# The gating unit's first mixes one product later, and another order of the output's block products, in a conditioned MLA and spatial gating layer

## The chip, the cores and the metric

The kernel runs on one core of one Trainium2 chip. What is measured is device time in microseconds (us) for one launch. Each profile is one execution on that chip. Its engines are called here by the names that the profile uses: PE is TensorE's matmuls, PEld its weight loads, DVE is VectorE, ACT is ScalarE, POOL is GpSimd, SP is SyncE, which issues most of the transfers. Times within the profile count from the first instruction.

## The reference

One layer of a decoder trunk for 512 tokens of width 2048, in float32:

```python
h = rmsnorm(x, attn_norm_g) * (1 + scale) + shift          # scale, shift, gate = silu(c) @ w_ada + b_ada
proj = h @ w_in                                            # 2048 x 13632, cut into
q_lat, kv_lat, k_rope, z_mla, u, v, z_sgu, g_mla, g_sgu    # 768, 512, 64 and six times 2048 columns
y_mla = attention(q_lat, kv_lat, k_rope) * silu(z_mla)     # 16 heads, causal, rotary
mixed = einsum('gts,bnsgd->bntgd', tril(w_spatial), rmsnorm(v) in chunks of 128 tokens) + b_spatial
y_sgu = u * mixed * silu(z_sgu)                            # 16 groups of 128 channels
merged = sigmoid(g_mla) * y_mla + sigmoid(g_sgu) * y_sgu
out = rmsnorm(x + gate * (merged @ w_out), final_norm_g)
```

Two places matter for this change: `mixed`, one 128 x 128 product for each group and chunk, and the last product, `merged @ w_out`, 512 x 2048 by 2048 x 2048, with the residual sum and the final norm behind it.

## The kernel before, in words

Every float32 product is made of three matmuls. Each operand is split into a high part (a copy that is rounded to the matmul's type, a cast on ScalarE) and a low part (the difference, on VectorE); high by high, high by low and low by high are summed in a bank of PSUM (`mm3`, lines 184 to 187). So every tile of weights is loaded, cast and subtracted before its matmuls, and the program writes out by hand in which order each engine does that.

**Four stages** follow each other: the first columns of the projection and the conditioning; the columns of v; the gates (266 block products); attention head by head; and the output product.

**Seven products in place of eight.** The v columns, the gates and half of the output's columns are computed with a scheme of seven block products over a cut into two by two blocks. The products are numbered 1 to 7. Products 1, 2, 3 and 4 are accumulated in one set of banks, in the order 1, 2, 3, 4, and copied out between (what is in the banks after each is needed); 6 and 7 in another; 5 in its own. Some weight operands are sums of blocks. Where a sum is not made on VectorE, a transfer makes it: it loads a block and adds it to what lies in the buffer. Such accumulating transfers are issued by POOL, plain loads by SP.

**The gates' stage.** A loop runs over 266 slots, one block product in each. Before it, a planner puts every other step into a slot and a phase (`on`, `place`, lines 817 to 840): a list of FIRST, EVAC, GATE, SPLIT and BACK steps is issued ahead of the slot's matmuls, MISC and LOAD behind them. Steps with a free choice are given a cost in us, and `place` takes the next slot whose sum on VectorE stays under a limit. The split of a slot's weights is issued two slots ahead. The gating unit's mix of two groups is a chain over several slots (lines 1078 to 1095): the spatial weights, their bias and the columns of v are loaded at `s_ - 3`; POOL zeroes the upper triangle at `s_ - 1` (`sgu_weights`, line 1057); ScalarE scales v by its norm (`sgu_scale`, line 1062), which needs `rv`, made in slot 4; PE makes the four products (`sgu_mix`, line 1067, in phase MISC); VectorE takes them from PSUM and adds the bias (`sgu_out`, line 1073). The first pair of groups planned is 14 and 15 (`p` = 7), at slots 1 to 12. Its neighbours in the queues: the accumulation for product 4 of the first pair of gates is issued by POOL in slot 3, phase LOAD, and is used in slot 9; small steps for the rotary angles (`rope_make`) are placed from slot 4 on; the conditioning's dot products (`gate_dot`) from two slots behind the pair's end; and so on through the stage.

**The output's stage.** Columns 1024 to 2047 are made first, plainly, in 16 granules of weights. Columns 0 to 1023 are made with products 1 to 7, four granules of weights for each product. `Stream` (from line 57) holds the list of all granules in the order of use. At each `get` it issues the low part of the next granule, the cast of the one after that, and then as many transfers, in the order of the list, as there are free buffers; it stops at the first that has none, or whose `after` granule has not been split. A granule's buffer is free when its low part has been issued. The buffers for plain loads are three, a fourth (`k0`, `k1`) from step 16 to step 24, and another (`ys2`) from step 27. A granule of product 3 is one load and one accumulation onto the same buffer (`both`). A granule of product 6, 2 or 4 has no buffer of that kind: product 6 uses a chain tile `ch0` to `ch3`, and a granule of 2 or 4 is that chain tile after one more accumulation (`chain_add`). All those accumulations are issued on POOL when the stream comes to them.

The steps 16 to 39 of the loop (from line 1980) are the 24 block products, each with 12 matmuls (`out_block`, line 1876; PE's lines there are called L1883). Copies of banks and the epilogue's steps hang on step numbers (`at_out`). Three of them: `hold` copies product 6's banks at step 23, the sum of 1 and 2 at step 31 (`y12`) and the sum of 1, 2 and 3 at step 35 (`y123`), each on ScalarE, line 1891; the next product on these banks has to wait until they are read. Product 5's first two granules are loaded early into other tiles and split at steps 26 and 27; its last two come through the stream. Product 5 is made last, for two rows of 128 tokens, the second cut into halves, in banks 2, 3 and 6 (`last_product`), while VectorE, ScalarE and POOL finish the other two rows.

## Time and profile before

| | |
|---|---|
| median of 3 runs | 1535.6 us (1534.37 to 1535.95) |
| the profiled execution, its own time | 1538.92 us |
| its span, from the first to the last instruction | 1537.2 us |
| mean granted PE clock | 0.997 of full speed |
| PE busy | 1517.3 us, 99% |
| PEld busy | 1412.9 us, 92% |
| VectorE busy | 1244.6 us, 81% |
| ScalarE busy | 808.6 us, 53% |
| POOL busy | 135.4 us, 9% |
| transfers | 346.48 MB, mean 225 GB/s |

How it is read: a row of the view in order of time has the start and the length in us, the engine, the line, the operation, what it writes and reads, and in square brackets the idle time of that engine before it, with what ended it. A row of the view of waits has who waited, for whom, the sum in us, how many times, and the longest. The chain of waits, followed back from the last instruction, lies on PE for 89% of the span; it leaves PE at the start, around 193 to 211 us, from 326 to 356 us, around 1082, 1340 and 1424 to 1449 us, and from 1473 us on. DMA rows give the time from issue to landing as least, median and greatest.

### The profile page before, as it was taken

What the parts mean: (1) busy time and instruction counts of PE and PEld (TensorE: products, weight loads), DVE (VectorE), ACT (ScalarE), POOL (GpSimd) and SP (SyncE); (2) the same over time, 40 slices, a digit from 0 to 9 for tenths busy, and PEclk for the clock granted to TensorE, in tenths of its full rate; (3) what the DMA queues carried; (4) which work ended last, traced back from release to release, by engine and by line L of the source; (5) the groups of instructions that cost most, each with busy time, mean ns of one, the idle gap of its engine ahead of it and who ended that gap; (6) DMA issues with size and microseconds to landing.
All of it is one profiled execution on the core that took longest, in us unless ns stands there. A gap on an engine that the chain in (4) does not pass through costs nothing.

```text
span 1537.2 us, 27419 instructions
## 1 busy us (share of the span) xinstructions
PE 1517.3 (99%) x10560; PEld 1412.9 (92%) x10560; DVE 1244.6 (81%) x1931; ACT 808.6 (53%) x1415; POOL 135.4 (9%) x158
## 2 busy tenths in 40 slices
PE   9999999999999999999999999999999999999996
PEld 7888988999999999999999999999888888888885
DVE  8989988767888888877787777777788888867886
ACT  4444566555545454454555646556655555542454
POOL 0000011010111110111111111111000000000022
PEclk9999999999999999999999999999999999999998
DMA  9978789778999998998888888888544334237694
GB/s 374 393 266 315 236 243 281 227 201 239 277 252 272 267 249 257 262 259 203 224 238 248 221 244 241 222 204 221 165 131 141 134 121 143 87 135 237 172 250 167
DMA packets 137894, 346.48 MB, mean 225 GB/s; under 512 B 15753, under 2 KB 40097, under 8 KB 133537
## 3 DMA queue, kind: packets, MB, share of 16 engines
q1 hardware_dynamic: 117010, 277.34, 52.2%
q0 software_dynamic: 20608, 67.12, 24.0%
q8 instruction: 83, 1.36, 0.4%
q14 instruction: 49, 0.40, 0.1%
q10 hardware_dynamic: 144, 0.26, 0.0%
HBM read 320.72 MB, written 23.94 MB: 224 GB/s over the span
## 4 chain that ended last, share of the span: by engine, by line
PE 89%; DMA 4%; DVE 3%; issue 2%; ACT 1%; POOL 0%; SPq 0%; DVEq 0%; ACTq 0%; POOLq 0%
PE ps L1511 15%; PE ps L1513 15%; PE ps L1512 15%; PE ps L185 10%; PE ps L186 10%; PE ps L187 10%; PE ps L709 7%; PE ps L1883 2%; DMA ch<-in_wo 1%; PE ps L1690 1%; PE ps L1071 1%; DMA wraw<-in_w 1%; DMA wraw<-in_wh 1%; DMA lat<-in_wv 1%; DVE ys L173 1%
## 5 line engine op out<-in xcount | busy, mean ns | idle before, releaser
L1511 PE MATMUL ps<-h,w0h 128*128 128x256 f32 x408 | 113.1, 277 | 2.0 <-DVE lat L173 2.0
L1511 PE MATMUL ps<-h,w2h 128*128 128x256 f32 x408 | 113.8, 279 | 0.0
L1513 PE MATMUL ps<-h,w2l 128*128 128x256 f32 x408 | 112.7, 276 | 0.0
L1512 PE MATMUL ps<-h,w0h 128*128 128x256 f32 x408 | 112.7, 276 | 0.0
L1512 PE MATMUL ps<-h,w2h 128*128 128x256 f32 x408 | 112.7, 276 | 0.0
L1513 PE MATMUL ps<-h,w0l 128*128 128x256 f32 x408 | 112.7, 276 | 0.0
L1511 PE MATMUL ps<-h,w1h 128*128 128x256 f32 x400 | 110.9, 277 | 0.0
L1513 PE MATMUL ps<-h,w1l 128*128 128x256 f32 x400 | 110.5, 276 | 0.0
L1512 PE MATMUL ps<-h,w1h 128*128 128x256 f32 x400 | 110.5, 276 | 0.0
L173 DVE TENSOR_TENSOR w0l<-raw,w0h 128x1024 fp32r<-128x1024 f32 x56 | 68.5, 1224 | 31.4 <-ACT w0h L897 30.6
L185 PE MATMUL ps<-h,w1h 128*128 128x512 f32 x218 | 86.6, 397 | 0.0
L187 PE MATMUL ps<-h,w1l 128*128 128x512 f32 x218 | 85.1, 390 | 0.0
L186 PE MATMUL ps<-h,w1h 128*128 128x512 f32 x218 | 85.0, 390 | 0.0
L173 DVE TENSOR_TENSOR w1l<-wraw,w1h 128x1024 fp32r<-128x1024 f32 x44 | 53.9, 1224 | 35.7 <-ACT w1h L897 35.7
L139 ACT CAST w0h<-wraw 128x1024 fp32r<-128x1024 f32 (+5 forms) x65 | 56.9, 883 | 47.8 <-issue 23.1
L875 POOL DMA_DIRECT2D wraw<-in_wh x55 | 49.3, 953 | 369.3 <-DVE w1l L173 154.2
L173 DVE TENSOR_TENSOR w2l<-wraw,w2h 128x1024 fp32r<-128x1024 f32 x46 | 56.3, 1223 | 30.6 <-ACT w2h L897 30.6
L1511 PEld LDWEIGHTS ps<-h,w0h 128*128 128x128 f32 x408 | 76.6, 188 | 2.1 <-issue 2.1
L185 PE MATMUL ps<-h,w0h 128*128 128x512 f32 x198 | 78.1, 394 | 0.0
L186 PE MATMUL ps<-h,w0h 128*128 128x512 f32 x198 | 77.2, 390 | 0.4 <-DVE h L176 0.4
L187 PE MATMUL ps<-h,w0l 128*128 128x512 f32 x198 | 77.5, 391 | 0.0
L1512 PEld LDWEIGHTS ps<-h,w2h 128*128 128x128 f32 x408 | 76.6, 188 | 0.5 <-issue 0.5
(496 smaller groups left out, 5494.2 us busy)
## 6 DMA issues: line engine op xcount, KB each, us to landing
raw<-in_wh SPq DMA_DIRECT2D x104, 512.0 KB, 7.0
wada<-in_wada SPq DMA_DIRECT2D x31, 1024.0 KB, 7.4
wraw<-in_wh POOLq DMA_DIRECT2D x55, 512.0 KB, 8.0
wraw<-in_wh SPq DMA_DIRECT2D x44, 512.0 KB, 6.5
raw<-in_wh POOLq DMA_DIRECT2D x36, 512.0 KB, 7.2
wraw<-in_wo SPq DMA_DIRECT2D x28, 512.0 KB, 3.7
half<-in_w SPq DMA_DIRECT2D x35, 256.0 KB, 5.8
wraw<-in_w SPq DMA_DIRECT2D x16, 512.0 KB, 8.4
```

What stands on the lines that cost most here:

```text
L139: self.nc.scalar.copy(self.hi[k][0][:, sl], src)
L173: DVE.tensor_tensor(out=out, in0=in0, in1=in1, op=op)
L185: PE.matmul(ps, ah, bh, start=start, stop=False)
L186: PE.matmul(ps, ah, bl, start=False, stop=False)
L187: PE.matmul(ps, al, bh, start=False, stop=stop)
L709: PE.matmul(psv[key][n], x_[:, tk], w_[:, sl], start=st and m == 0, stop=ch == 7 and m == 2, skip_group_check=True)
L875: q_.dma_start(t, wh[h, n, q // 10 - 1], **eng)
L1071: PE.matmul(ps[:, n], v[:, n], wr[:, q], start=True, stop=True)
L1511: PE.matmul(ps[:, :256], wH[:, cols[c]], xh, start=c == 0 and first, stop=False, skip_group_check=True)
L1512: PE.matmul(ps[:, :256], wH[:, cols[c]], xl, start=False, stop=False, skip_group_check=True)
L1513: PE.matmul(ps[:, :256], wL[:, cols[c]], xh, start=False, stop=c == 7, skip_group_check=True)
L1883: PE.matmul(ps[:, o:o + m], x_[:, tk], w_[:, sl], start=c == 0 and e == 0 and p in "165", stop=c == 7 and e == 2, skip_group_check=True)
```

## The change

There are two edits. In the planner of the gating unit, the start for the first pair of groups (14 and 15) and for the next (0 and 1) goes from slot 4 to 5 and with it all their loads, the mask, the scales, the mixes and what is placed from their ends. In the output, the list of granules is written out: the fourth granule of product 7 comes behind product 2 instead of before it, and the matmuls of product 5's first granule, for all three of its parts, are issued at step 36, before product 4's first granule. The copy `y12` goes from step 31 to step 30. The stream adds its granules in the new order, so its transfers, casts and low parts follow it.

```diff
-    for p in "1672345":
-        for i in range(2 if p == "5" else 0, 4):
-            if p in "157":
...
+    blocks = [(p, int(i)) for p, i in "10 11 12 13 60 61 62 63 70 71 72 20 21 22 23 73 30 31 32 33 40 41 42 43 52 53".split()]
+    for p, i in blocks:
+        if p in "157":
...
-    sgu_end, s_, e_ = {}, 4, -2
+    sgu_end, s_, e_ = {}, 5, -2
     for p in (7, 0, 1, 2, 3, 4, 5, 6):
-        s_ = max(s_, 4 if p in (0, 7) else base[1 + 5 * p + 1] + 2)
+        s_ = max(s_, 5 if p in (0, 7) else base[1 + 5 * p + 1] + 2)
...
-        at_out(31, lambda n=n: hold("y12", n, pbank["y"][n], tp, "sig"))
+        at_out(30, lambda n=n: hold("y12", n, pbank["y"][n], tp, "sig"))
         at_out(35, lambda n=n: hold("y123", n, pbank["y"][n], tp, "sig"))
+
+    half = S // 2
+    lasts = (2, 0, 0, S), (3, 1, 0, half), (6, 1, half, half)
+    wl = early
+
+    def last_block(i, b, n, o, w):
+        if i == 0:
+            pbank[b] = bank_at(b)
+        out_block("5", i, n, wl[i], pbank[b], o, w)
...
-            p, i = "167234"[s // 4 - 4], s % 4
+            p, i = blocks[s - 16]
...
+            if s == 36:
+                for part in lasts:
+                    last_block(0, *part)
...
-    wl = early + [get(seq[40]), get(seq[41], 0)]
+    wl = wl + [get(seq[40]), get(seq[41], 0)]
...
-    def last_product(n, b, o, w):
-        ps = bank_at(b)
-        for i in range(4):
-            out_block("5", i, n, wl[i], ps, o, w)
-        return ps[:, o:o + w]
+    def last_product(part):
+        for i in range(1, 4):
+            last_block(i, *part)
+        b, n, o, w = part
+        return pbank[b][:, o:o + w]
...
-    ps = [last_product(0, 2, 0, S), last_product(1, 3, 0, half), last_product(1, 6, half, half)]
+    ps = [last_product(part) for part in lasts]
```

## The prediction

> Blocks are named product/granule: 3/3 is granule 3 of product 3. Times are us of the profiled execution.

> **What bounds the kernel now.** First the page, then the idle time of TensorE by what ended it:

> ```profile
> span 1537.2 us, 27419 instructions
> ...
> PE ps L1883 <- ACT sig L1891: 3.0, 2, 2.2
> PE ps L1511 <- DVE lat L173: 2.0, 1, 2.0
> ```

> TensorE stands still for 5 us in the two places that are edited, and hardly elsewhere. That is the most that hiding the waits themselves can bring. Next, ScalarE and TensorE in time around the output's waits:

> ```profile
> 1486.30 1.05 ACT L139 CAST w2h<-wraw 128x1024 fp32r<-128x1024 f32 x1 [3.13 <-DMA wraw<-in_wo]
> ...
> 1488.76 1.05 ACT L139 CAST w1h<-wraw 128x1024 fp32r<-128x1024 f32 x1 [0.79 <-DMA wraw<-in_wo]
> 1489.71 1.07 ACT L1891 COPY sig<-ps 128x512 f32<-128x512 f32 x2
> ...
> 1490.35 0.50 PE L1883 MATMUL ps<-w2h,b 128*128 128x512 f32 x1 [0.77 <-ACT sig L1891]
> ...
> 1494.22 1.05 ACT L139 CAST w2h<-ys 128x1024 fp32r<-128x1024 f32 x1 [1.96 <-DMA ys<-in_wo]
> ...
> 1498.05 1.05 ACT L139 CAST w1h<-ch 128x1024 fp32r<-128x1024 f32 x1 [2.78 <-DMA ch<-in_wo]
> ...
> 1502.13 1.04 ACT L139 CAST w0h<-ch 128x1024 fp32r<-128x1024 f32 x1 [0.91 <-DMA ch<-in_wo]
> 1503.08 1.07 ACT L1891 COPY sig<-ps 128x512 f32<-128x512 f32 x2
> ...
> 1503.71 0.50 PE L1883 MATMUL ps<-w1h,b 128*128 128x512 f32 x1 [2.19 <-ACT sig L1891]
> ...
> 1506.56 0.39 PE L1883 MATMUL ps<-w0h,b 128*128 128x512 f32 x1
> ...
> 1512.00 0.39 PE L1883 MATMUL ps<-w1h,b 128*128 128x512 f32 x1
> ...
> 1509.23 1.05 ACT L139 CAST w1h<-ch 128x1024 fp32r<-128x1024 f32 x1 [2.24 <-PE ps L1883]
> ```

> TensorE waits for the two bank copies (L1891), but the copies stand on ScalarE behind a weight cast, and the casts wait for a transfer. These are the accumulating transfers that POOL issues, for 3/0 to 3/3 and 4/0 to 4/3: their casts run at 1486.30, 1488.76, ..., 1494.22 (3/3), 1498.05, 1502.13 (4/1), ..., 1509.23 (4/3). The last names TensorE as its releaser, but it too keeps the rhythm of POOL's queue. So **what is late is POOL's queue of accumulations**: 2.46 us apart at first (1486.30 to 1488.76), up to 4.1 later.

> The end depends on it as well. Behind 4/3's cast follow on VectorE, in order, its low part, a corner row, the low parts of 5's last granules, and then the first use of product 4's banks:

> ```profile
> 1514.72 0.62 PE L1883 MATMUL ps<-V,b 128*128 128x512 f32 x2
> ...
> 1525.80 0.28 PE L1883 MATMUL ps<-V,g 128*128 128x256 f32 x1
> ...
> 1516.05 0.68 DVE L173 TENSOR_TENSOR sig<-ps,gbc 128x512 f32<-128x512 f32 x1
> ```

> The first is the start of product 5, the second TensorE's last matmul, the third that use: 6.8 us after the cast at 1509.23. A block is (1512.00 - 1506.56)/2 = 2.72 long and fills one bank in its first half, so product 4's first bank is full near 1512.00 + 1.36 + 0.3 = 1513.7 (4/3 starts at 1512.00; the 0.3 is the last matmul's way through the array): TensorE has 2.4 us to spare here: **finishing it earlier alone brings nothing; 4/3's landing sets the end.**

> **Output, what the change gains.** Moving 7/3 behind 2/3 puts a block of 2.72 on other banks in front of 3/0. The copy of product 2's banks now stands behind 3/0's cast (1486.30) instead of 3/1's, so it begins near 1487.4 and is over before 3/0 starts at 1489.4: 0.77 gone, with the slow first matmuls 1.07 (1490.35 less 1489.28 by the rhythm of 2.72). 5/0 ahead of 4/0 is 11.1/4 = 2.8 of matmuls on banks 2, 3 and 6 (1514.72 to 1525.80 is four granules); it covers the 2.19 if all else stays. No matmul is added.

> **Output, what it moves.** The stream of weights issues its transfers in the order of the blocks, on SP, and has POOL accumulate in that order too.

> ```profile
> 1476.58 0.33 SPq L98 DMA_DIRECT2D ys<-in_wo  x1
> ...
> 1478.46 0.84 POOL L284 DMA_DIRECT2D wraw<-in_wo  x1 [13.30 <-DMA wraw<-in_wo]
> ...
> 1482.00 0.85 POOL L284 DMA_DIRECT2D ys<-in_wo  x1 [0.44 <-DVE yp L173]
> 1482.53 2.94 POOL L284 DMA_DIRECT2D ch<-in_wo  x3
> ...
> 1484.12 1.22 DVE L151 TENSOR_TENSOR w0l<-ch,w0h 128x1024 fp32r<-128x1024 f32 x1
> ```

> Now 7/3 frees its buffer before product 2 begins; 3/3's load goes to a fourth buffer at 1476.58, its accumulation to POOL at 1482.00, and those of product 4 right behind (1482.53). With 7/3 four blocks later its buffer is held four blocks longer. Going through the buffers by hand: 3/2 takes the fourth one (1476.58), and 3/3 has none until 7/3 is split, which is now where 2/3's split was, 1484.12 + 1.22 = 1485.3. So 3/3's load leaves SP 8.8 us later, at 1485.4. POOL takes its queue in order: 3/3's accumulation waits for that load, and **4/0 to 4/3 are queued behind it**, though 2/0 to 2/2 have long freed their buffers. 7/3's own load goes out four blocks later too and lands well before use; product 2's accumulations wait for product 6's splits as before. Both cost nothing.

> How late is the chain then? In order: the landing time of the load at 1476.58, of one at 1488.64, of the accumulation at 1478.46, and what moved from 1482 to 1492:

> ```profile
> DMA to landing us min/median/max: 4.9/4.9/4.9
> ...
> DMA to landing us min/median/max: 9.7/9.7/9.7
> ...
> DMA to landing us min/median/max: 7.7/7.7/7.7
> ...
> q0 software_dynamic: 566, 2.06, 105.7%
> ```

> In those 10 us only POOL's queue moved, 0.206 MB/us. Three accumulations of 0.52 MB (3/0 to 3/2) empty it near 1481 + 7.6 = 1488.6, so the load is not held up for 9.7; between 4.9 and 9.7 I take 5.3: it lands at 1490.7. The accumulation goes out at 1490.8. Its landing: 7.7 from an empty queue; I take 8.2, since SP's loads for 5/2, 5/3 and the rows run beside it: 1499.0, against 1494.1. The four that follow were 2.46 apart alone and (1509.23 - 1494.22)/4 = 3.75 beside those loads. Part of the loads will have gone while POOL's queue stood empty; I take 3.2. Then 4/1 lands at 1505.4, 4/3 at 1511.8, its cast at 1511.9: **+2.7**.

> TensorE: 3/3 starts 2.2 after its landing (cast 1.05, low part 1.22) at 1501.2, 5/0 ends at 1506.9, 4/0 waits for the copy behind 4/1's cast: 1505.5 + 1.58 (1502.13 to 1503.71) = 1507.1. Product 4's first bank is full 9.95 later (three blocks, 0.13 for the slow start, half a block and 0.3), at 1517.0; the epilogue reaches it at 1516.05 + 2.7 = 1518.7. So the landing, not TensorE, decides: +2.7. Bounds: if load and accumulation were so quick that 3/3 landed before 1495.4, no wait is left and the bank is full at 1503.1 + 9.95: -3.0. With 6.0 for the load, 8.6 and 3.75: 1500.1 + 15.0 = 1515.1, that is +6.

> Without a wait 3/3 would start at 1497.6 (now it does at 1490.35 + 2.85 + 2 x 2.72 = 1498.6, less the 1.07), so TensorE stands idle 3.6 before it. After the 2.19 of now the next block took 1506.56 - 1503.71 = 2.85, 0.13 more than usual, and I count that. [...]

> **Gating unit.** Here a later block's weights are late:

> ```profile
> 338.66 1.23 DVE L173 TENSOR_TENSOR w2l<-wraw,w2h 128x1024 fp32r<-128x1024 f32 x1 [1.17 <-ACT w2h L897]
> 340.55 1.06 POOL L1059 TENSOR_SCALAR_AFFINE_SELECT wsr<-wsr 128x256 f32<-128x256 f32 x1 [10.05 <-DMA wsr<-in_wsT]
> 341.55 0.85 POOL L875 DMA_DIRECT2D wraw<-in_wh  x1
> ...
> 348.03 0.28 DVE L180 TENSOR_SCALAR rx<-rx,vec 128x128 f32<-128x128 f32 x1
> ...
> 349.40 0.75 DVE L173 TENSOR_TENSOR lat<-ps,lat 128x256 f32<-128x256 f32 x2
> ...
> 351.09 0.35 ACT L1015 COPY lat<-ps 128x256 f32<-128x256 f32 x1
> 352.64 1.05 ACT L897 CAST w0h<-wraw 128x1024 fp32r<-128x1024 f32 x1 [1.20 <-DMA wraw<-in_wh]
> 353.72 1.22 DVE L173 TENSOR_TENSOR w0l<-wraw,w0h 128x1024 fp32r<-128x1024 f32 x1 [1.56 <-ACT w0h L897]
> 354.87 0.74 DVE L176 SCALAR_TENSOR_TENSOR cosT<-ps,vec,bsr 128x512 f32<-128x512 f32 x1
> ...
> 355.99 0.41 DVE L173 TENSOR_TENSOR lat<-lat,ps 128x256 f32<-128x256 f32 x1
> ...
> 356.55 0.36 PE L1511 MATMUL ps<-h,w0h 128*128 128x256 f32 x1 [1.98 <-DVE lat L173]
> ...
> DMA to landing us min/median/max: 3.4/6.0/8.7
> ```

> The mask select (340.55) waits for its weights, and product 4's accumulation (341.55) stands behind it on POOL. One slot later the select comes after it; the accumulation then goes when its buffer is read, 338.66 + 1.23 = 339.9, and lands some 1.5 earlier. The cast runs when ScalarE is free, 351.4 instead of 352.64. On VectorE the planner fills the place of the mix's output (354.87) and two small steps, 1.12 until 355.99, with five rotary steps, 1.37 (348.03 to 349.40). So the subtraction begins 1.0 earlier: a wait of 1.0 is left of 1.98. Against it: the v load moves behind two weight loads on SP, to about 340.7. Its landing took 3.4 and, beside weight loads, 8.7 (the last row: both of them). At 8.7 it holds ScalarE until 349.4, 1.3 later than it wants, and costs 0.4. I take **-0.7**, bounds -1.0 and +0.4. The later gate dot products, each a slot on, fill slots with room; nothing waits for them.

> **Sum**: -0.7 + 2.7 = +2.0. The profiled execution took 1538.9 (span 1537.2), 3.3 over the median; I add to the median: 1537.6.

> **Rivals.** (1) The waits are hidden and the queue catches up: gating -1.0, output -2.5, 1532.1. For it: TensorE's waits are real and covered in the order of blocks. Against: 3/3 would have to land by 1495.4, 10.0 after its load's issue, where 4.9 + 7.7 make 12.6. (2) Quick rows throughout: 4.9, 7.7 and 2.46 give 4/3 at 1508.0, but 5/0 then ends at 1506.0 and the bank is full at 1516.0: output 0, 1534.9. (3) Slower by over 0.2%: the loads for 5/2, 5/3 and the rows share the engines with the late accumulations all the way, 3.75 apart, gating 0: up to +6, with +4 as the middle 1539.6. It decides once 4/3 lands after 1512.2.

> **Numbers.** A measurement of this kernel tells 0.2%, 3.1 us, from no change. Forecast 0.45 (own range 1536 to 1539), rival 1 0.15, rival 2 0.15, rival 3 0.25. Faster is rival 1: 0.15. Slower is rival 3 and 0.06 of the forecast: 0.31. Same: 0.54. The range 1533.0 to 1541.0 leaves out about half of rival 1 and the end of rival 3.

> **What would show it.** Right: no wait for L1891 before 3/0; TensorE idle before 3/3, released by the split of a weight tile; 3/3's accumulation issued near 1491; L1511's wait near 1 us, its cast no longer released by a transfer. Wrong: 3/3's accumulation issued before 1487, 4/3's cast before 1509, or a mix that TensorE waits for.

## The result and the profile after

The changed kernel took 1542.69, 1545.21 and 1548.47 us, against a median of 1535.32 for the kernel before: a ratio of 1.0067, 95% interval [1.0042, 1.0091]. (A fourth execution, 2561.6 us at a granted clock of 0.556, is left out.) Two later sets gave 1.0061 [1.0048, 1.0074] and 1.0058 [1.0046, 1.0070]. So it is slower, by some 9 us, where the forecast was +2.0 and "no change". Its profiled execution is its fastest.

First the page and the waits of TensorE after (who waits for whom, sum in us, times, longest):

```profile
span 1540.9 us, 27414 instructions
PE ps L1883 <- ACT w2h L139: 3.3, 1, 3.3
PE ps L1883 <- DVE w0l L151: 1.1, 2, 0.8
...
PE ps L1511 <- DVE lat L173: 0.9, 1, 0.9
```

The waits for the bank copies are gone and the one at L1511 is half of that in the first trace of before, as predicted. In their place stands one of 3.3 before 3/3, and another, 0.77, for its low part. In order of time:

```profile
1484.50 2.94 SPq L98 DMA_DIRECT2D wraw<-in_wo  x2
...
1489.84 0.85 POOL L284 DMA_DIRECT2D wraw<-in_wo  x1 [9.19 <-DVE w0l L151]
1490.37 3.82 POOL L284 DMA_DIRECT2D ch<-in_wo  x4
...
1499.08 1.04 ACT L139 CAST w2h<-wraw 128x1024 fp32r<-128x1024 f32 x1 [9.28 <-DMA wraw<-in_wo]
...
1500.18 0.49 PE L1883 MATMUL ps<-w2h,b 128*128 128x512 f32 x1 [3.31 <-ACT w2h L139]
...
1505.60 0.63 PE L1883 MATMUL ps<-V,b 128*128 128x512 f32 x2
1508.42 0.40 PE L1883 MATMUL ps<-w1h,b 128*128 128x512 f32 x1
...
1511.36 1.06 ACT L139 CAST w1h<-ch 128x1024 fp32r<-128x1024 f32 x1 [2.33 <-PE ps L1883]
...
1513.91 1.23 DVE L151 TENSOR_TENSOR w0l<-ch,w1h 128x1024 fp32r<-128x1024 f32 x1 [0.17 <-PE ps L1883]
...
1519.75 0.68 DVE L173 TENSOR_TENSOR sig<-ps,gbc 128x512 f32<-128x512 f32 x1
```

3/3's load leaves at 1484.50 and its accumulation at 1489.84, with product 4's four behind it; the cast starts at 1499.08 and TensorE, idle since 1496.9, at 1500.18. The block of 3/3 then takes 1505.60 - 1500.18 = 5.42 where a block is 2.72, 5/0 takes 2.82, and 4/0 starts at 1508.42 against 1503.71 before. From here on TensorE is the one that is waited for: 4/3's cast (1511.36) for the tile that 4/0 read, its low part (1513.91) for the one that 4/1 read. Product 4's banks are first used at 1519.75, 3.70 later than before, and the span is 3.7 longer. Why 3/3 took twice its time is in the granted clock (columns: length, busy time of TensorE, its weight loads, VectorE, ScalarE, POOL, then the clock):

```profile
1497.94:1501.35 3.41, 0.49 (x1) 0.19 (x1) 1.19 (x2) 1.04 (x1) 0.00 (x0) 1.00 1.08 256
1501.35:1504.76 3.41, 3.32 (x8) 2.65 (x9) 2.55 (x4) 2.34 (x3) 0.00 (x0) 0.50 1.07 211
```

Behind the idle stretch stand 3.41 us at half clock. Full clock then holds to 1532.07, 27.31 us or eight times 3.41, and half clock comes back behind TensorE's last matmul. So the clock of this trace is read in windows of 3.41 us.

### The profile page after: what moved, and what is told of

It reads as the page before. It is cut to its first block, busy times and chain, and to the rows that moved or that the text cites. A ratio compares the mean times of both kernels' runs of the same rounds, so it can differ in the third digit from the quotient of the medians.

```text
span 1540.9 us, 27414 instructions
## 1 busy us (share of the span) xinstructions
PE 1520.3 (99%) x10560; PEld 1415.3 (92%) x10560; DVE 1245.0 (81%) x1931; ACT 808.3 (52%) x1415; POOL 135.3 (9%) x158
## 3 DMA queue, kind: packets, MB, share of 16 engines
q8 instruction: 83, 1.36, 0.3%
## 4 chain that ended last, share of the span: by engine, by line
PE 91%; DVE 4%; DMA 3%; ACT 1%; issue 1%; SPq 0%; DVEq 0%; POOL 0%; ACTq 0%; POOLq 0%
PE ps L1511 15%; PE ps L1513 15%; PE ps L1512 15%; PE ps L185 10%; PE ps L187 10%; PE ps L186 10%; PE ps L709 7%; PE ps L1883 3%; PE ps L1690 1%; PE ps L1071 1%; DMA lat<-in_wv 1%; DVE sig L173 1%; DVE ys L173 1%; DMA raw<-in_wv 1%; PE ps L1654 1%
## 5 line engine op out<-in xcount | busy, mean ns | idle before, releaser
L1511 PE MATMUL ps<-h,w0h 128*128 128x256 f32 x408 | 113.1, 277 | 0.9 <-DVE lat L173 0.9
L1511 PE MATMUL ps<-h,w2h 128*128 128x256 f32 x408 | 113.8, 279 | 0.0
L1511 PE MATMUL ps<-h,w1h 128*128 128x256 f32 x400 | 110.8, 277 | 0.0
L173 DVE TENSOR_TENSOR w0l<-raw,w0h 128x1024 fp32r<-128x1024 f32 x56 | 68.5, 1223 | 30.9 <-ACT w0h L897 30.1
L875 POOL DMA_DIRECT2D wraw<-in_wh x55 | 49.1, 949 | 379.5 <-DVE w1l L173 146.3
L139 ACT CAST w0h<-wraw 128x1024 fp32r<-128x1024 f32 (+5 forms) x65 | 56.9, 883 | 47.2 <-issue 23.0
L173 DVE TENSOR_TENSOR w1l<-wraw,w1h 128x1024 fp32r<-128x1024 f32 x44 | 53.9, 1224 | 34.2 <-ACT w1h L897 34.2
L173 DVE TENSOR_TENSOR w2l<-wraw,w2h 128x1024 fp32r<-128x1024 f32 x46 | 56.3, 1223 | 30.0 <-ACT w2h L897 30.0
L1511 PEld LDWEIGHTS ps<-h,w0h 128*128 128x128 f32 x408 | 76.6, 188 | 1.1 <-issue 1.1
```

Of the source, the lines that this page charges most:

```text
L139: self.nc.scalar.copy(self.hi[k][0][:, sl], src)
L173: DVE.tensor_tensor(out=out, in0=in0, in1=in1, op=op)
L875: q_.dma_start(t, wh[h, n, q // 10 - 1], **eng)
L1511: PE.matmul(ps[:, :256], wH[:, cols[c]], xh, start=c == 0 and first, stop=False, skip_group_check=True)
```

## The experiments

Each kernel was timed in five rounds beside the kernel before, in four sets: e1 to e4; e5 to e7; b1, g1, o1, o2; e8, e9, g2, o3. A ratio holds against the before of its own set (medians 1535.3, 1535.2, 1535.7, 1535.0).

| kernel | what it is | median us | ratio to before, 95% |
|---|---|---|---|
| b1 | before itself | 1535.36 | 0.9998 [0.9990, 1.0007] |
| e1, e9 | the change itself | 1543.62, 1543.85 | 1.0061, 1.0058 (above) |
| e2 | gating edit alone | 1536.10 | 1.0010 [1.0001, 1.0019] |
| g1 | e2, first load of v kept | 1537.00 | 1.0008 [0.9999, 1.0016] |
| g2 | e2, all first loads kept | 1536.14 | 1.0008 [0.9999, 1.0017] |
| e3 | output order alone | 1542.41 | 1.0052 [1.0039, 1.0064] |
| e4 | change, 5/0 at the end | 1543.18 | 1.0063 [1.0049, 1.0077] |
| e5 | change, 7/3 in its old place | 1537.08 | 1.0015 [1.0007, 1.0024] |
| e6, e8 | change, 5/0 computed twice | 1545.59, 1543.11 | 1.0070 [1.0056, 1.0083], 1.0055 [1.0039, 1.0070] |
| e7 | change, a buffer more | 1539.33 | 1.0024 [1.0015, 1.0033] |
| o2 | e7, late loads held back | 1537.43 | 1.0013 [1.0004, 1.0022] |
| o3 | o2 without the gating edit | 1535.52 | 1.0004 [0.9995, 1.0013] |
| **o1** | **before, late loads held back** | **1533.11** | **0.9981 [0.9972, 0.9989]** |

**Was the profile of before an ordinary one?** The kernel before, unchanged, for a second trace.

> The kernel before itself, for a second trace. The runs so far bring up a rival to the prediction's reading: that the profiled execution of before, at 1538.9 us 3.4 over the median of the others, is no ordinary one, and that the two waits read in it are not there in the others. By this rival (D) the trace shows less than 0.5 us of idle time at line 1511 near 355 us (the trace with the output's edit alone, which has the same gating code, has none above 0.4) and less than 0.4 before 3/0 (the trace with the gating edit alone, which has the same output code, has none). If the first trace was ordinary: 1.5 to 2.3 and 0.6 to 0.9 again. The wait before 4/0 is about 2 us in either case.

Its page, TensorE's waits, product 4's cast and the subtraction ahead of its matmuls in the gates, and 4/3's cast:

```profile
span 1533.6 us, 27419 instructions
...
PE ps L1883 <- ACT sig L1891: 1.5, 1, 1.5
...
351.00 1.05 ACT L897 CAST w0h<-wraw 128x1024 fp32r<-128x1024 f32 x1
...
354.35 0.41 DVE L173 TENSOR_TENSOR lat<-lat,ps 128x256 f32<-128x256 f32 x1
...
1505.62 1.05 ACT L139 CAST w1h<-ch 128x1024 fp32r<-128x1024 f32 x1 [2.43 <-DMA ch<-in_wo]
```

The rival holds: this execution is 3.6 shorter, has no wait at L1511, none before 3/0, and one of 1.5 before 4/0 (2.19 in the first trace, about 2 expected). The transfer that the gating edit was to bring forward landed in time, and the cast waits for nothing. Two of the three waits that the edits aim at are not in this trace. Of the other traces with the gating start of before, e3's, o1's and o3's have waits of 0.3 to 1.1 in all at L1511.

**Which edit costs what.** The expectations set accounts of the loss against each other. Theory A: TensorE, idle before 3/3 and at half clock behind it, sets the end. Theory B, the forecast's: 4/3's landing sets it. Theory C: 5/0 in front of 4/0 is the loss. e2, e3, e4 and e5 make parts of the change:

```diff
 e2:  before, with  sgu_end, s_, e_ = {}, 5, -2  and  max(s_, 5 if p in (0, 7) ...
 e3:  the change, with both of these back at 4
 e4:  the change, without  if s == 36: ... last_block(0, *part) ;  last_product: for i in range(4)
 e5:  the change, blocks "... 70 71 72 73 20 21 22 23 30 ...", y12 at step 31
```

> The gating unit's edit alone, the output's blocks as before. Both theories: 0.9 us faster than before (the changed kernel's trace is 0.86 us ahead at the first output block), so 1534.4 with 1533.9 to 1535.0. If it is slower than before, part of the loss comes from the gating unit, and neither theory covers that.

> The order of the output's blocks alone, the gating unit as before. Both theories: 0.9 us slower than the changed kernel, so about 12 us slower than before (1547.7, if the changed kernel is at 1546.8). If it comes out at or below the changed kernel, the two edits work on each other.

> The changed kernel with 5/0 back at the end, so that only 7/3 is moved in the output. Theory A (TensorE sets the end): the idle time before 3/3 and the half clock behind it stay, 4/0 starts when the copy of 3's banks is over instead of 2.8 us of 5/0 later, and the kernel is 1.0 to 2.8 us faster than the changed one. Theory B (4/3's landing sets the end): 5/0 costs nothing where it stands, so no change (within 0.5 us of the changed kernel).

> The changed kernel with 7/3 back in its old place, so that only 5/0 is moved in the output (and the gating unit's edit stays). Theory A: 3/3's load is not held, no idle time before 3/3, full clock; 0.77 us idle before 3/0 is back; 4/0 starts 2.8 us behind 3/3's end instead of 2.4, and the end keeps its place: 1534.0 to 1536.0, so 10 us or more faster than the changed kernel. Theory C (the 2.8 us of 5/0 in front of 4/0 are the loss, since they delay 4's blocks): 2 to 3 us slower than before.

e2 missed: the gating edit costs 0.8 where 0.9 was to be gained. e3 missed in turn: without that edit the kernel is faster than the change, not slower. Nearly all of the loss is the output's order (e3, +7.1), and in it 7/3's move: with 7/3 alone (e4) the loss stays, with 5/0 alone (e5) it is 1.9, of which 0.8 belongs to the gating edit. e4 missed what theory A expected, 1.0 to 2.8 faster, by the medians (1543.18 and 1543.62), but its five executions lie from 1542.06 to 1546.90, and the traces tell more. In all seventeen VectorE comes to product 4's banks 5.7 to 5.8 us after it has started 4/3's low part, and the span ends 21.1 to 21.3 later. So what this low part waits for sets the end. In the traces of the change (after, e1, e9) and of e3, e4, e6 and e8 that is TensorE, which still reads the tile (1513.91 above); 4/0 starts 2.96 earlier in e4's than in e1's, and its span is 2.8 shorter. In both traces of before and in those of e2 and e5 it is 4/3's cast, in b1 and e5 behind its landing. Theory A therefore holds for the changed kernel. In e5, which missed A's forecast, the trace has no wait before 4/0, so 5/0 covers it as meant; nothing is gained, since the landing decides there.

The start of 4/0, 4/3's low part and the first use of product 4's banks in b1:

```profile
1499.89 0.50 PE L1883 MATMUL ps<-w1h,b 128*128 128x512 f32 x1 [1.50 <-ACT sig L1891]
...
1506.70 1.23 DVE L151 TENSOR_TENSOR w0l<-ch,w1h 128x1024 fp32r<-128x1024 f32 x1 [0.93 <-ACT w1h L139]
...
1512.43 0.68 DVE L173 TENSOR_TENSOR sig<-ps,gbc 128x512 f32<-128x512 f32 x1
```

In the first trace after, 4/0 starts 8.5 later (1508.42): 3/3 starts 4.7 later, its block takes 2.7 longer, 5/0 takes 2.8, and the 1.7 that b1 loses in front of 4/0 are saved. TensorE was 1.2 ahead of the low part in b1, so 7.2 of this reach it (1513.91), and the span is 7.3 longer.

**The hold on 3/3's buffer, and the loads beside it.**

```diff
 e7:  the change, and
+        if s == 28:
+            ws.more_raws([(dpp, "ys3")])
-        at_out((20, 20, 35, 32)[n], row_load, n)
+        at_out((20, 20, 35, 35)[n], row_load, n)
 o2:  e7, and
+        if s == 32:
+            ws.look = 3
 o1:  before, with row_load at 35, 35 and ws.look = 3 from step 32
 o3:  o2, with the gating unit's start back at 4
```

With `look` at 3 the stream issues 5/2 and 5/3 behind the rows' loads, and the first of those waits for a buffer that a granule of product 3 still holds; so all four loads leave SP later. No arithmetic changes.

> The changed kernel with one more buffer for weights (the tile of row 3's input, whose load moves from block 32 to block 35), so that 3/3's load starts at once instead of behind 7/3's split. Theory A: 3/3's load issues about 7 us earlier and its accumulation lands about 1491 instead of 1499; no idle time before 3/3, no half clock, 4/1 ends 6 us earlier: the gains are left, and the kernel is 1 to 3 us faster than before (1532.5 to 1534.5). Theory B: the landings of 4/0 to 4/3 come 3 us earlier with it, so also faster than before, by up to 2; it differs from A in that the clock in the stretch does not matter. Theory C (5/0 ahead of 4/0 is the loss): 2 us slower than before.

The times from issue to landing of the accumulations, with the first and last issue, for e7 and the wait left in it:

```profile
L284 POOL DMA_DIRECT2D ch<-in_wo x4: 1187/1694/2202, 1486.5 to 1488.1; - x4
L284 POOL DMA_DIRECT2D wraw<-in_wo x2: 841/848/855, 1478.3 to 1479.6; - x2
...
DMA to landing us min/median/max: 6.2/11.9/21.1
...
1505.16 0.50 PE L1883 MATMUL ps<-w1h,b 128*128 128x512 f32 x1 [1.85 <-ACT sig L1891]
```

No idle time before 3/3 is left, no half clock, and 4.2 us of the change's loss are gone by the medians (8.3 to 4.1 over before): the hold is the largest part of it. But theories A and B, which had it faster than before, and C, 2 us slower, all missed: it is 4.1 slower by the medians, 1.0024 of before. The eight land from 1478.3 + 6.2 = 1484.5 to 1488.1 + 21.1 = 1509.2, 3.5 apart: 3/3's load and that of 5/2, which now goes out at 1485.2, run beside them, and the wait before 4/0 is back. That led to the next three.

> The kernel before, with four loads of the output's last steps held back: rows 2 and 3 of the input and the weights of 5/2 and 5/3 leave SP only when 3/3's buffer is free, near 1497 instead of 1488.6 to 1491. Theory S (the accumulations of 3/3 to 4/3 come 3.3 to 4.1 us apart instead of 2.5 because these loads share the transfer engines, and their landing makes the waits): 4/0 lands 1.5 to 2 us earlier, the wait before 4/0 shrinks from about 2 to about 1 us, 4/3 lands up to 2 us earlier, and the kernel is 1 to 2 us faster than before (1533.3 to 1534.3). Rival (accumulations have that spacing by themselves, by POOL's queue): no change, or slower where the held-back loads are now waited for.

The same view for the second trace of before, and then for o1:

```profile
L284 POOL DMA_DIRECT2D ch<-in_wo x4: 855/1360/1864, 1480.5 to 1483.6; - x4
L284 POOL DMA_DIRECT2D wraw<-in_wo x3: 841/841/855, 1475.1 to 1477.6; - x3
...
DMA to landing us min/median/max: 7.7/12.2/22.0
```

```profile
L284 POOL DMA_DIRECT2D ch<-in_wo x4: 855/1363/1744, 1480.0 to 1483.7; - x4
L284 POOL DMA_DIRECT2D wraw<-in_wo x3: 841/841/855, 1475.2 to 1477.6; - x3
...
DMA to landing us min/median/max: 6.3/10.4/16.3
...
1494.21 1.75 SPq L1932 DMA_DIRECT2D ys<-in_xn  x2
1496.01 1.04 SPq L98 DMA_DIRECT2D wraw<-in_wo  x2
```

Before: from 1475.1 + 7.7 = 1482.8 to 1483.6 + 22.0 = 1505.6, 3.3 apart. In o1, with the four loads from 1494.21 on: 1481.5 to 1500.0, 2.6 apart. The last lands 5.6 earlier, no wait of the output is left on TensorE, and the kernel is faster than before. Theory S is right, and its forecast (1533.3 to 1534.3) was a little too careful. All eleven executions lie between 1531.77 and 1533.78. **o1 beats both kernels** without either edit.

> The changed kernel with the further buffer for 3/3 and, in addition, the four late loads held back until 3/2's and 3/3's buffers are free. Theory S: 3/3 lands near 1492 instead of 1495.3 and 4/0 near 1495 instead of 1499.7, no idle time before 3/3 nor above 1 us before 4/0, and the kernel is 2 to 4 us faster than with the further buffer alone (1539.3), so 1535.3 to 1537.3 with the gating edit's 0.8 in it. Theory C (5/0 in front of 4/0 delays the end by itself): within 1 us of the kernel with the further buffer alone.

> The output's new order with the further buffer and the late loads held back, without the gating unit's edit. Beside it stands the old order with the late loads held back (1533.1, no wait left on TensorE in its trace). Theory C (once no wait is left, 5/0 in front of 4/0 only delays 4's blocks, on which the end hangs): 2 to 3 us slower than that, 1535 to 1536. If the order is neutral once its loads come in time: 1532.6 to 1534.

o2 is 1.9 below e7 by the medians, at the edge of what was expected. o3, beside it without the gating edit, is the new order with the further buffer and the late loads held back: 1.0004 of before, and 2.4 over o1 by the medians. The two stood in different sets, so it is a comparison through before. The size is that of theory C, 2 to 3, but o3's trace does not show its cause:

```profile
1506.62 1.05 ACT L139 CAST w1h<-ch 128x1024 fp32r<-128x1024 f32 x1 [2.81 <-DMA ch<-in_wo]
...
1507.70 1.22 DVE L151 TENSOR_TENSOR w0l<-ch,w1h 128x1024 fp32r<-128x1024 f32 x1 [0.87 <-ACT w1h L139]
```

TensorE has no wait left in the output, but 4/3's low part waits for its cast and this for the landing, 1506.5 against 1500.0 in o1; 3/3's accumulation leaves POOL at 1483.84 against 1479.51, so this order still makes the accumulations late. TensorE is through with 4/1 at 1506.97: without the late landing the low part could start some 0.7 earlier (an estimate from these rows), and 5/0's 2.8 would be the next limit. The run does not separate the two.

**The gating edit's 0.8.**

```diff
 g1:  e2, and  on(s_ - (4 if p == 7 else 3), LOAD, v_load, 2 * p)
 g2:  e2, and the same start for sgu_load, bias_load and v_load
```

> The gating unit's edit alone, with one step kept where it was: the first load of v (pair 7) stays in slot 1, ahead of the two weight loads. Theory V (the edit's loss is the load of v, which lands 5 to 7 us later behind those weights and holds ScalarE's scale of v up, so that product 4's cast and low part come 1.5 to 2 us later): the scale waits for nothing, and the kernel is 1.0 to 2.0 us faster than with the gating edit alone (1536.1), so 1534.1 to 1535.1. Rival (the rotary steps that now stand in front of product 4's low part and of the subtraction on VectorE are the loss): within 0.4 us of the gating edit alone.

> The gating unit's edit alone, with all loads of the first pair (the spatial weights, the bias and v) kept in slot 1, so that SP's order is that of before up to product 4; only the mask, the scale, the mix and what follows are a slot later. Theory V (the moved loads are the edit's loss): product 4's accumulation is issued 1 to 2 us earlier than in before as the edit intends, no wait above 0.5 us on TensorE near 352 to 357, and the kernel is at 1534.5 to 1535.5: no slower than before (1535.4), and 0.6 to 1.6 below the gating edit alone (1536.1). Rival (the later steps on VectorE are the loss): 1536 or more.

The moved load shows in the second trace of the changed kernel, ScalarE's scale of v and two waits of TensorE:

```profile
349.62 1.28 ACT L1065 ACTIVATE lat<-lat,rv 128x128 f32<-128x128 f32 x4 [1.83 <-DMA lat<-v_d]
...
353.16 0.38 PE L1511 MATMUL ps<-e,w1h 128*128 128x256 f32 x1 [1.56 <-ACT lat L1015]
...
357.10 0.36 PE L1511 MATMUL ps<-h,w0h 128*128 128x256 f32 x1 [0.94 <-DVE lat L173]
```

The scale stands until the load lands; the copy behind it (L1015) is late, and TensorE waits for that. This wait for the load was 0.44 in the first trace after, 1.83 here, and 4.80 in o2's, where the mix too waits for the scale. It is in eight of the ten traces with the moved load, and not in e2's and e5's. TensorE's waits between 330 and 362 us sum to 0.7 to 4.1 in these ten and to 0 to 2.0 in the five with the start of before. But keeping the loads in place did not bring the time back: g1 and g2 are at 1.0008, like e2. In g1's trace the mix waits for the mask instead (0.6); in g2's neither waits, and what is left is this:

```profile
350.10 1.05 ACT L897 CAST w0h<-wraw 128x1024 fp32r<-128x1024 f32 x1
...
353.64 0.41 DVE L173 TENSOR_TENSOR lat<-lat,ps 128x256 f32<-128x256 f32 x1
...
354.20 0.36 PE L1512 MATMUL ps<-h,w0h 128*128 128x256 f32 x1 [0.73 <-DVE lat L173]
```

From cast to subtraction are 3.54 us, in the second trace of before 3.35 (354.35 - 351.00); no landing ends either cast's wait, so there is no wait that the edit could take away, and one of 0.73 stands at the end. o1's and o3's traces, with the start of before, have 0.7 for the same releaser, so this wait alone proves nothing. Theory V, that the moved loads are the edit's loss, is refuted as the whole cause; what the rest is, later steps on ScalarE and VectorE or another thing, stays open.

**What the half clock costs.**

```diff
 e6, e8:  the change, with
-            if s == 36:
+            if s in (35, 36):
                 for part in lasts:
                     last_block(0, *part)
```

> The changed kernel itself once more, for a second trace and more times. Theory A (3/3's load comes late because 7/3 holds its buffer, TensorE then idles about 3.5 us before 3/3 and runs at half clock behind that, and TensorE, no longer POOL's queue, sets the end): the idle time before 3/3 is 3.3 to 3.8 us again, and executions that take longer have a longer stretch at a lower clock behind it; a span of 1546.8 at a mean clock of 0.994 against 1540.9 at 0.996 says about 6 us more at half clock. Theory B (the forecast's: the landing of 4/3 sets the end, the clock is hidden): longer executions have later landings of 3/3 to 4/3, by as much as they are longer, at the same clock.

> The changed kernel, but 5/0 is computed twice: 24 matmuls more (2.8 us) in front of 3/3, into the banks that the second 5/0 starts anew; the output is the same. They fill most of the idle time and change no load. Theory A: idle before 3/3 about 0.7 us, full clock in 3/3, so 4/0 starts 2.7 us earlier than in the changed kernel in its shortest execution and more in the others: 2.7 us faster than its shortest, and 4 to 8 us faster by the medians. Theory B: no change (within 0.5 us), as the loads land when they did. If the extra matmuls themselves count on the path, up to 2.8 us slower.

> The kernel that computes 5/0 twice, once more, beside the changed kernel on the same chip. Its first trace had the full clock throughout, where four traces of kernels with the idle time before 3/3 had half clock for 3.41 us (one) or 6.83 us (three); yet its median, 1545.6, was not below the changed kernel's 1543.6 of another set of runs. Theory A (half clock for one or two windows of 3.41 us costs 1.7 or 3.4 us): full clock again before the tail, and 1.5 to 3.5 us faster than the changed kernel beside it. Rival E (the 24 extra matmuls take back what the clock gives, or the end waits for the landings all the same): within 1 us of it or slower, with the clock at full speed.

> The changed kernel beside it. By both theories 3.3 to 4.6 us idle before 3/3 and half clock behind it for 3.41 or 6.83 us, the median between 1543 and 1547.

The changed kernel's second trace, in three windows of the clock:

```profile
1499.01:1502.42 3.41, 0.00 (x0) 0.00 (x0) 0.00 (x0) 0.92 (x1) 0.00 (x0) 1.00 1.06 265
1502.42:1505.83 3.41, 2.76 (x6) 1.88 (x7) 2.96 (x4) 1.63 (x3) 0.00 (x0) 0.50 1.07 213
1505.83:1509.25 3.42, 3.42 (x10) 2.64 (x9) 2.14 (x3) 3.36 (x7) 0.00 (x0) 0.50 1.06 210
```

Here it is two windows, 6.83 us at half clock, as in the traces of e3, e4 and e9; the first trace had one. That is a loss of TensorE time of up to 1.7 or 3.4 (half of 3.41 and 6.83, an estimate), and part of why executions of one program differ. The idle time is 4.4 here, over the expected 3.3 to 3.8, since 3/3's accumulation took 10.1 to land instead of 9.1: both what theory A names and what theory B names vary from execution to execution. With the extra matmuls (18 by the pages' counts, 10578 against 10560, not 24), e6's trace keeps the full clock, but e8's does not:

```profile
1504.63:1508.05 3.42, 1.17 (x6) 0.60 (x5) 1.67 (x2) 1.04 (x1) 0.00 (x0) 1.00 1.08 230
1508.05:1511.46 3.41, 3.41 (x10) 2.63 (x9) 2.23 (x4) 3.33 (x6) 0.00 (x0) 0.50 1.06 209
```

So the expectation that 5/0 twice keeps the clock up failed, and by the medians (1543.11 beside 1543.85 in the set that holds both) nothing is won. Nor is e6's trace typical of its kernel: its mean clock is 0.997, that of the other four executions 0.994 or 0.995. It takes 10.2 from 3/2's end to 4/0's start (1498.23 to 1508.39), where the first trace after takes 11.7 (1496.71 to 1508.42); but it came 1.5 later out of the gates, so the two spans are alike (1541.0 and 1540.9). No run changes the clock alone. But in the changed kernel's traces the end waits for TensorE, so what the half clock takes from TensorE there reaches the end: some 1.7 in the first trace after, an estimate from its rows, since 4/3 had landed at 1509.8, 4.1 before its low part.

## Why the prediction was right or wrong

**The gains: wrong at the base.** The steps "0.77 gone", "covers the 2.19" and the gating unit's "1.0 is left of 1.98" were read from an execution that the text itself called 3.3 over the median, and the sum, counted from that execution, was then added to the median. The second trace of before has 0, 1.5 and 0 for these three. The difference, 0.77 + 0.69 + 1.98 = 3.4, is nearly all of the 3.6 by which the two spans differ: that execution was long by the waits that were to be removed. The edits did to the waits what was said (none at L1891, 0.9 at L1511, 5/0 covering 4/0's wait in e5); in an ordinary execution there was little to remove. Counted from b1 the forecast would have been some +5.4 (2.0 + 3.4, an estimate); the spans of b1 and after are 7.3 apart.

**The hold on the buffer: right, and right in size.** 3/3's load at 1484.50 (predicted 1485.4), 4.8 to land (5.3), accumulation issued at 1489.84 (1490.8), landed 9.1 later (8.2), idle time before 3/3 of 3.3 (3.6). The trace runs 0.9 ahead of before there, which accounts for most of the differences.

**"So the landing, not TensorE, decides": wrong, the step that failed in the output.** Product 4's accumulations landed 2.7 apart ((1509.8 - 1499.0)/4), not 3.2, and 4/3 was there at 1509.8 instead of 1511.8. TensorE was later than its term: 4/0 at 1508.42 instead of 1507.1 although the trace runs ahead, since 3/3's block took 5.42 and not 2.85. And the sum looked only at when the bank is full, 9.95 behind 4/0's start. The end hangs on 4/3's low part, and this waited for the tile that TensorE was still reading: it starts at 1513.91, and VectorE comes to the banks 5.84 later, 11.33 behind 4/0's start. So TensorE's 1517.0 became 1519.75, past the landing's 1518.7. In the trace of before, TensorE's 2.4 to spare were likewise 1.0 (the tile free at 1509.28, the low part at 1510.32). For the 0.3 in these terms the rows show 0.20 to 0.25: ScalarE's copy of a bank starts at 1467.89 in the first trace of before and at 1484.67 after, 0.47 and 0.43 behind the start of the last matmul that it waits for (1467.42, 1484.24), and the next matmul starts 0.23 behind that. The profiled execution, +3.8 on that of before, has these terms; the other traces of the change have two windows at half clock and more idle time. e7, where the hold is gone, shows 4.2 of the 8 to 9 us.

**The half clock: a loss that the sum has no term for.** The forecast has the idle time before 3/3, and behind it counts 0.13 for a slow start; in the first trace after, 3/3's block took 5.42 where 2.85 was counted, with 3.41 us at a clock of 0.50. Of the traces with 3/3's late load and no filler one has one window at half clock and four have two. The trace of before shows a lower clock behind an idle stretch too: TensorE's last matmul starts at 1525.80, and the mean clock from 1526 to 1537 is 0.66.

**The gating unit: -0.7 predicted, +0.8 measured by the medians, +1.5 [+0.2, +2.9] by the ratio (e2).** The load of v was seen to move behind two weight loads (expected 340.7, issued 339.5) and costed at 0.4 at most; in eight of ten traces it held ScalarE, for 0.44 to 4.80. As g1 and g2 show, that is not all of it. And the transfer whose lateness was the gain is not late in an ordinary execution.

**The rivals.** Slower by over 0.2% came true, at 0.25 the second likeliest, but not by the mechanism named: loads beside the late accumulations. That mechanism did appear, in e7 (3.5 apart) and in the old order (3.3), and to take it away was the gain of o1. Rival 1 needed the waits of the first trace and 3/3 landed by 1495.4; it landed at 1499.0. Rival 2 had the load right (4.8), but not the accumulation (9.1, not 7.7). Of what was to show the forecast wrong, "a mix that TensorE waits for" is in g1's, o2's and e8's traces. But all the signs that were to show it right are in the first trace after, so they could not tell it from what happened.

## What to carry to other kernels

Take a second trace of the kernel before counting a wait as a gain: an execution that is longer than the median may be longer by waits that the others do not have. When an item of a stream is moved back, follow the buffer that it holds to the next load, and then every queue behind that load; the hold cost some 4 us, where an ordinary execution had 1.5 of waits to hide in the output. Ask on which instruction the end hangs, here the low part of the last granule, and follow both of its inputs: the landing, and the engine that still reads its tile. Where transfers make the waits, look first at which loads beside them are early without need: holding back four of them gained 0.2% where reordering the matmuls lost 0.6%.

## What was not expected of the hardware

How little idle time brings half clock. The windows of 3.41 us of two more traces, one with the old output order (g2, behind the wait before 4/0) and one behind waits in the gates (o2), and the same place in the first trace of before, which kept its clock:

```profile
1497.60:1501.01 3.41, 1.53 (x7) 0.93 (x6) 2.01 (x3) 2.78 (x6) 0.00 (x0) 1.00 1.06 279
1501.01:1504.42 3.41, 3.41 (x9) 2.63 (x8) 2.20 (x2) 1.29 (x3) 1.32 (x1) 0.50 0.88 253
```

```profile
351.66:355.07 3.41, 1.32 (x8) 1.16 (x8) 0.00 (x0) 2.58 (x6) 0.00 (x0) 1.00 0.71 249
355.07:358.48 3.41, 2.48 (x11) 2.48 (x12) 2.22 (x4) 2.77 (x4) 0.00 (x0) 0.50 0.26 77
```

```profile
1502.16:1505.57 3.41, 1.86 (x8) 1.56 (x9) 2.36 (x3) 2.61 (x5) 0.72 (x1) 1.00 1.04 278
1505.57:1508.98 3.41, 3.41 (x17) 2.83 (x16) 3.08 (x4) 1.05 (x1) 0.61 (x1) 1.00 0.28 102
```
